# Hybrid decoder layer: the order of the norms at the seam between the first projections and the pairs, and of the first loads

## The chip, the cores and the metric

The kernel runs on one core of a Trainium2 chip. The metric is the device time of one execution in microseconds; a profiled execution shows where it goes. TensorE (PE in the profile) multiplies, VectorE (DVE) and ScalarE (ACT) prepare its operands and empty its banks, GpSimd (POOL) does side work and issues some transfers, and SyncE (SP) issues most transfers.

## The reference

One decoder layer on 512 tokens with 2048 features, in float32. What matters here is its front end:

```python
xn = rms_norm(x, attn_norm_g)          # per token, over 2048 features
proj = xn @ w_in                       # gq gk gv gg ga fq fk fv fg ff mq mg
...                                    # eight GLA heads, four FoX heads
mn = rms_norm(mem, mem_norm_g)         # 256 memory tokens
mk, mv = split(mn @ w_mem_kv)
...                                    # four heads of cross-attention over mem
h = x + (headnorm(o) * gate) @ w_out
y = h + relu(rms_norm(h) @ w_up) ** 2 @ w_down
```

The two norms that the change touches are those of x (one factor for each of 512 tokens) and of mem (one for each of 256). A norm's factor is a scale of a row, so the kernel multiplies with x and mem as they come and applies the factor when a result leaves its bank.

## The kernel before

Every product is made of three matmuls of 128 by 128 by 512 in a rounded format (`mm3`, L174 to L178): each operand is split into a high part (a copy on ScalarE) and a low part (the rest, a subtraction on VectorE).

The kernel is one sequence of stages on TensorE. The first projects two groups of columns, gk and gq (`project`, L232): eight rounds, in each of them two weight tiles and two tiles of x. The last of the sums of squares of x (xacc, L208) is ready long before its end. Then come four *pairs* (L513 to L515): `in_pair(n, c)` makes one half of the contraction (c) of two groups of 512 columns (n = 0: the GLA values, n = 1: the FoX queries and keys), in the order n, c = (0,0), (1,0), (0,1), (1,1). The text calls them first to fourth pair. A pair is a two-by-two block product in seven products instead of eight (Strassen with Winograd's sums): products p in the order 1, 5, 6, 3, 7, 2, 4 (L256), and each p is two steps q of 12 matmuls, so a pair has 14 steps or 168 matmuls. A weight block of a step is loaded (L311), perhaps combined with another block (`minus`, L472), and split into `hl` on ScalarE and VectorE (L367). There are four `hl` buffers, taken in turn: the split for a step starts when TensorE has left the step four before it. Names such as `hl_hl_in_51` say p = 5, q = 1.

After the last step of a product `evict` (L484) takes its two banks to the output o, with the factor of x's norm, r_x: on ScalarE (L492) the first time a place is written in the first two pairs, and on VectorE (L490) otherwise. Products 1, 6, 7 and 4 go on adding in the same two banks, so product 6 may start only when the eviction after product 1 is done; products 5 and 3 share another two.

Sums of blocks of x are an operand of products 5, 6, 3 and 7. For the first half of the contraction (c = 0) they are made during `project` and lie in sh (high) and sl (low). For c = 1 they are made by `x_sums(1)` (L427) in tiles xs (loads) and st (results) and parked in device memory by GpSimd (x_op, L442). During the second pair `next_sums` (L448) loads them back into sl, each when its product of the second pair is done, and splits them at once: the load, a copy on ScalarE, a subtraction on VectorE.

Beside that run the sums of squares of mem: 16 loads memT (L509), 16 squares on ScalarE (L219), 15 additions on VectorE (L220). `token_rstd` (L222) then multiplies with a column of ones (ss_x for x, ss_mem for mem; four and two small matmuls, L226), and `rsqrt` (L116) makes the factor in five small VectorE and two ScalarE operations. The program has, in this order: ss_x and r_x; x_sums(0); the squares of mem, then x_sums(1); ss_mem and its factor; the four pairs. The factor of mem is first used when mem's projections leave their banks, long after the pairs.

Two pools of buffers are shared: three `ta` tiles serve xraw, xs and memT in turn, four `tb` tiles serve the squares and st. Small banks of TensorE come from the pool of four `a` banks, in turn: gq has all four, then ss_x, ss_mem, product 5 of the first pair.

Where an instruction stands in its engine's queue is not the order of the text alone. A scheduler orders the program by priorities: `tc.high_priority(offset)` moves what it holds ahead, `urgent()` (L280) by twice the usual offset. Each engine then takes its queue strictly in order, SP's queue of transfers included: a transfer that waits for a buffer holds up all behind it.

Of the kernel before, what the change touches and what calls it, by code (L numbers as in the profile page):

```python
# [9 lines left out]
F32 = mybir.dt.float32  # L10
# [8 lines left out]
NT = S // 128  # L19
NK = D // 128  # L20
M = 256
MT = M // 128
# [16 lines left out]
AHEAD = 3000  # L39
# [8 lines left out]
def hybrid_layer(  # L48
# [17 lines left out]
    nc = tc.nc  # L66
    V, A, G, T = nc.vector, nc.scalar, nc.gpsimd, nc.tensor
# [26 lines left out]

    colt = const.tile([128, 68], F32, name="colt")
    with tc.high_priority(offset=AHEAD):
        nc.sync.dma_start(colt, cols)
    g_attn, g_mem, g_out, g_mlp = (colt[:, 16 * i : 16 * i + 16] for i in range(4))
    g_fq, g_fk, g_mq, g_mk = (colt[:, 64 + i : 65 + i] for i in range(4))

# [30 lines left out]
    def empty(evict, p, acc):  # L131
        traced = nc.cur_bb.bb.instructions
        last = traced[-1]
        with tc.high_priority(offset=2 * AHEAD):
            evict(p, acc)
        start = next(i for i in reversed(range(len(traced))) if traced[i] is last) + 1
        for engine in (V.engine, A.engine):
            emptied.extend([(turns["step"], i) for i in traced[start:] if i.engine == engine][-1:])
# [19 lines left out]
    def wtile(src, name, n=1024, parts=1):  # L158

        with tc.high_priority(offset=AHEAD):  # L160
            raw = wraw(turns["raw"] % 3, f"raw_{name}")
            turns["raw"] += 1
            both = hl_in(name, n_hl)
            hi, lo = both[:, :n], both[:, 1024 : 1024 + n]
            for i in range(parts):
                cs = slice(i * n // parts, (i + 1) * n // parts)
                nc.sync.dma_start(raw[:, cs], src[:, cs])
                A.copy(hi[:, cs], raw[:, cs])
                V.tensor_sub(lo[:, cs], raw[:, cs], hi[:, cs].bitcast(F32))
        return hi, lo  # L170
# [23 lines left out]
    def tmp(name, tag, n=512, dt=F32):  # L194
        return tp.tile([128, n], dt, tag=tag, name=name, bufs=TAGS[tag])
# [26 lines left out]
    def token_rstd(acc, n, name):  # L222

        ss = abank(f"ss_{name}")
        for t in range(n):
            T.matmul(ss[:, t : t + 1], lhsT=acc[:, t * 128 : t * 128 + 128], rhs=one_c, start=True, stop=True)  # L226
        r = const.tile([128, n], F32, name=f"r_{name}")
        rsqrt(r, ss[:, :n], n, 1.0 / D, name)
        return r


    def project(*groups):  # L232

        banks = [[(abank if i else gbank)(f"{g}_{t}") for t in range(NT)] for i, g in enumerate(groups)]
        for kp in range(NK // 2):
            for ps, group in zip(banks, groups):
                wh, wl = wtile(w_in[GROUPS.index(group), kp], f"{group}{kp}", parts=1 if kp else 2)
                for kk in range(2):
                    k = 2 * kp + kk
                    ah, al = x_tile(k)  # L240
                    for t in range(NT):
                        cs = slice(kk * 512 + t * 128, kk * 512 + t * 128 + 128)
                        mm3(ps[t], wh[:, cs], wl[:, cs], ah, al, k == 0, k == NK - 1)
        return [p for ps in banks for p in ps]
# [35 lines left out]
    def urgent():  # L280
        return tc.high_priority(offset=2 * AHEAD)
# [122 lines left out]


    kq = project("gk", "gq")
    xrstd = token_rstd(xacc, NT, "x")
    kTs = bigt(0, [128, NT, 512], "kTs")
    qTs = bigt(1, [128, NT, 512], "qTs")
    with urgent():  # L410
# [36 lines left out]

    def next_sums(n):  # L448
        hi, lo = sh[:, n, :, :], sl[n // 2][:, n % 2, :, :]
        nc.sync.dma_start(lo.bitcast(F32), x_op[n])  # L450
        A.copy(hi, lo.bitcast(F32))
        V.tensor_sub(lo, lo.bitcast(F32), hi.bitcast(F32))


    places = [[(1, 1), (1, 2)], [(0, 0), (0, 1)], [(0, 2), (1, 0)]]
# [1 line left out]
    class Pair(Weights):  # L457
# [16 lines left out]
        def left(self, p, j, u):  # L474
# [5 lines left out]
            at = u * 128 + (256 if p == 4 else 0)  # L480
            return xh[k][:, at : at + 128], xl[k][:, at : at + 128]

    def in_pair(n, c):
        def evict(p, acc):  # L484
            r, col = WHERE[p]
            for u in range(2):
                t = 2 * r + u
                dst = o[:, t, n * 1024 + col * 512 : n * 1024 + col * 512 + 512]
                if c or p in (3, 7, 2):
                    V.scalar_tensor_tensor(dst, acc[u], rs_x(t), dst, op0=ALU.mult, op1=ALU.add)  # L490
                else:
                    A.activation(dst, acc[u], AF.Copy, scale=rs_x(t))  # L492

        def after(p, acc):
            empty(evict, p, acc)
            if (c, n) == (0, 1) and p in SUMS:
                with tc.high_priority(offset=AHEAD):
                    next_sums(SUMS[p])

        multiply(Pair(n, c), after)  # L500

# [2 lines left out]

    macc = spare[:, 3072 : 3072 + M]
    with tc.issue_after(turned_kq[0].ins), tc.issue_after(turned_kq[1].ins):
        for k in range(NK):
            mt = tmp(f"memT_{k}", "ta", M)
            nc.sync.dma_start(mt, memT[k])  # L509
            add_squares(macc, mt, k == 0, f"mem{k}")  # L510
        x_sums(1)
    mrstd = token_rstd(macc, MT, "mem")
    for c in range(2):  # L513
        for n in range(2):
            in_pair(n, c)  # L515
    blocks.close()
    n_hl = 2
    turns["raw"] = 0
# [1059 lines left out]
```

## Time and profile before

| | us |
|---|---|
| median of 3 runs | 2128.58 |
| their range | 2126.21 to 2132.4 |
| the profiled execution | 2126.06 |
| its span, first to last instruction | 2124.0 |
| first matmul | 5.97 |
| first pair starts | 97.21 |
| fourth pair ends | 263.5 |

The profiled execution lies 0.15 below the lowest of the three runs. A row of the timeline gives the start, the time, engine, line, operation, output and inputs, the form, and in brackets the idle time before it and what ended that. A row of the chain gives start, length, engine and output. A row of a wait gives who waited for whom, the total, how often, and the longest. The windows give the busy time of each engine in a stretch.

### The profile page before, as it was taken

The page shows a single profiled execution, that of the slowest core. Times are in us where ns is not written, and L with a number is a line of the kernel's source. Part 1 is how long each engine was busy: PE and PEld are TensorE (multiplying, and loading weights), DVE is VectorE, ACT ScalarE, POOL GpSimd, SP SyncE. Part 2 cuts the span into 40 slices and gives each one's busy share as a digit, 9 for nine tenths or more (in the row PEclk, how much of TensorE's full clock was granted, in tenths as well). Part 3 has the DMA queues.
Part 4 walks back from the last instruction along what each step waited for, and adds up shares of the span by engine and source line. Part 5 has one row for each costly group of instructions (what it writes and reads, how often), then busy time and mean ns, then how long its engine had stood idle before and what let it go on. Part 6 is the DMA issues. An engine that isn't in the chain of part 4 may idle for free.

```text
span 2124.0 us, 25538 instructions
## 1 busy us (share of the span) xinstructions
PE 2100.5 (99%) x9746; PEld 1733.4 (82%) x9746; DVE 1615.4 (76%) x1747; ACT 1133.3 (53%) x1607; POOL 152.1 (7%) x220
## 2 busy tenths in 40 slices
PE   8999999999999999999999999999999999999999
PEld 7777878887788788888888888888888888888887
DVE  6579888764664899977777777778968868777875
ACT  6454364434563565755555555556646546556543
POOL 0012000000000022100000000000100000000000
PEclk9999999999999999999999999999999999999999
DMA  7355342121224666353353353355677668668653
GB/s 264 97 164 168 118 139 93 60 70 60 85 91 143 237 256 216 112 208 120 131 206 119 130 207 119 129 208 199 207 208 236 176 196 254 168 187 268 182 174 129
DMA packets 78755, 347.09 MB, mean 163 GB/s; under 512 B 9305, under 2 KB 13401, under 8 KB 57130
## 3 DMA queue, kind: packets, MB, share of 16 engines
q1 hardware_dynamic: 58778, 274.95, 37.1%
q0 software_dynamic: 19856, 70.53, 12.5%
q8 instruction: 76, 1.25, 0.2%
q14 instruction: 45, 0.37, 0.1%
HBM read 271.52 MB, written 73.92 MB: 163 GB/s over the span
## 4 chain that ended last, share of the span: by engine, by line
PE 95%; DVE 2%; DMA 1%; ACT 1%; issue 1%; SPq 0%; DVEq 0%; ACTq 0%
PE acc_up L177 9%; PE acc_up L178 9%; PE acc_up L176 9%; PE acc_dn L178 9%; PE acc_dn L177 9%; PE acc_dn L176 9%; PE acc_in L177 2%; PE acc_in L176 2%; PE acc_in L178 2%; PE acc_out L177 2%; PE acc_out L178 2%; PE acc_out L176 2%; PE gg L176 1%; PE gg L178 1%; PE gg L177 1%; PE ut L1394 1%
## 5 line engine op out<-in xcount | busy, mean ns | idle before, releaser
L367 DVE TENSOR_TENSOR hl_up<-raw_up,hl_up 128x1024 fp32r<-128x1024 f32 x224 | 273.0, 1223 | 141.0 <-ACT hl_up L367 139.6
L367 DVE TENSOR_TENSOR hl_dn<-raw_dn,hl_dn 128x1024 fp32r<-128x1024 f32 x224 | 272.8, 1222 | 125.0 <-ACT hl_dn L367 124.7
L367 ACT CAST hl_up<-raw_up 128x1024 fp32r<-128x1024 f32 x224 | 235.0, 1050 | 204.4 <-PE acc_up L178 136.0
L367 ACT CAST hl_dn<-raw_dn 128x1024 fp32r<-128x1024 f32 x224 | 234.7, 1053 | 195.5 <-PE acc_dn L178 146.5
L315 DVE TENSOR_TENSOR raw_dn<-raw_dn,raw_dn 128x2048 f32<-128x2048 f32 x64 | 146.3, 2286 | 0.4
L315 DVE TENSOR_TENSOR raw_up<-raw_up,raw_up 128x2048 f32<-128x2048 f32 (+1 forms) x62 | 140.6, 2267 | 0.0
L367 ACT CAST hl_out<-raw_out 128x1024 fp32r<-128x1024 f32 x56 | 58.0, 1050 | 48.8 <-PE acc_out L178 21.4
L1492 ACT COPY m<-acc_dn 128x512 f32<-128x512 f32 x96 | 55.7, 587 | 43.0 <-PE acc_dn L178 42.9
L1493 POOL DMA_DIRECT2D hd<-m x48 | 41.5, 865 | 515.5 <-ACT m L1492 515.5
L367 DVE TENSOR_TENSOR hl_out<-raw_out,hl_out 128x1024 fp32r<-128x1024 f32 x56 | 72.5, 1306 | 6.6 <-ACT hl_out L367 6.2
L367 ACT CAST hl_hl_in<-spare 128x1024 fp32r<-128x1024 f32 x31 | 32.3, 1050 | 51.3 <-DVE spare L472 30.0
L1386 POOL DMA_DIRECT2D op<-u x32 | 17.1, 535 | 559.5 <-ACT u L1395 554.6
L1409 ACT ACTIVATE z<-z,rstd 128x512 f32<-128x512 f32 x48 | 32.2, 716 | 44.9 <-DVE z L1458 44.9
L176 PE MATMUL acc_in<-hl_hl_in,sh 128*128 128x512 f32 x128 | 50.9, 400 | 2.8 <-ACT o L492 2.8
L176 PE MATMUL gg<-ahi_x,hl_gg 128*128 128x512 f32 x128 | 53.5, 418 | 0.0
L177 PE MATMUL acc_in<-hl_hl_in,sh 128*128 128x512 f32 x128 | 51.1, 399 | 0.0
L178 PE MATMUL acc_in<-hl_hl_in,sl 128*128 128x512 f32 x128 | 50.8, 397 | 0.0
L176 PE MATMUL acc_up<-hl_up,left0h 128*128 128x512 f32 x128 | 50.5, 394 | 0.0
L176 PE MATMUL acc_up<-hl_up,left5h 128*128 128x512 f32 x128 | 50.5, 394 | 0.0
L176 PE MATMUL acc_up<-hl_up,left1h 128*128 128x512 f32 x128 | 50.5, 394 | 0.0
L176 PE MATMUL acc_up<-hl_up,left2h 128*128 128x512 f32 x128 | 50.5, 394 | 0.0
L177 PE MATMUL acc_dn<-hl_dn,left 128*128 128x512 f32 x128 | 50.0, 391 | 0.4 <-DVE hl_dn L367 0.3
(542 smaller groups left out, 6245.2 us busy)
## 6 DMA issues: line engine op xcount, KB each, us to landing
raw_up<-in_w_up_dram SPq DMA_DIRECT2D x64, 1024.0 KB, 6.2
raw_dn<-in_w_down_dram SPq DMA_DIRECT2D x64, 1024.0 KB, 6.9
hd<-m POOLq DMA_DIRECT2D x48, 512.0 KB, 6.5
raw_out<-in_w_out_dram SPq DMA_DIRECT2D x16, 1024.0 KB, 5.8
op<-u POOLq DMA_DIRECT2D x32, 512.0 KB, 4.2
op<-s POOLq DMA_DIRECT2D x24, 512.0 KB, 3.1
spare<-in_w_pair_dram SPq DMA_DIRECT2D x16, 512.0 KB, 4.7
raw_in<-in_w_pair_dram SPq DMA_DIRECT2D x16, 512.0 KB, 4.1
```

The source lines that it names most:

```text
L176: T.matmul(ps, lhsT=ah, rhs=bh, start=start, stop=False, skip_group_check=on)
L177: T.matmul(ps, lhsT=ah, rhs=bl, start=False, stop=False, skip_group_check=on)
L178: T.matmul(ps, lhsT=al, rhs=bh, start=False, stop=stop, skip_group_check=on)
L315: V.tensor_sub(dst, a, b)
L367: turns["made"] = made = A.copy(hi, part), V.tensor_sub(lo, part, hi.bitcast(F32))
L1386: nc.gpsimd.dma_start(down_op[c][i][:, half * 1024 : half * 1024 + 1024], tile)
L1394: T.transpose(tps[:, m * 128 : m * 128 + 128], z[:, t * 512 + m * 128 : t * 512 + m * 128 + 128], ident)
L1409: A.activation(dst, src, AF.Relu, scale=rstd[:, 2 * row + t : 2 * row + t + 1])
L1492: A.copy(st[:, t * 512 : t * 512 + 512], acc[t])
L1493: nc.gpsimd.dma_start(dst, st.rearrange("p (t n) -> p t n", t=2), accum_op=ALU.add)
```

## The change

Five edits. The gains `colt` go out on GpSimd's queue instead of SP's. `project` asks for the first tile of x of a round ahead of that round's weights. The norm of x is put under `urgent`. The loads, squares and additions of mem stand behind the first pair in the program, and ss_mem with its factor behind all four. `next_sums` issues its load when its product is done, as before, but copy and subtraction are held back until the next product is done.

```diff
-        nc.sync.dma_start(colt, cols)
+        nc.gpsimd.dma_start(colt, cols)
...
         for kp in range(NK // 2):
             for ps, group in zip(banks, groups):
+                x_tile(2 * kp)
                 wh, wl = wtile(w_in[GROUPS.index(group), kp], f"{group}{kp}", parts=1 if kp else 2)
...
     kq = project("gk", "gq")
-    xrstd = token_rstd(xacc, NT, "x")
+    with urgent():
+        xrstd = token_rstd(xacc, NT, "x")
...
     def next_sums(n):
         hi, lo = sh[:, n, :, :], sl[n // 2][:, n % 2, :, :]
-        nc.sync.dma_start(lo.bitcast(F32), x_op[n])
-        A.copy(hi, lo.bitcast(F32))
-        V.tensor_sub(lo, lo.bitcast(F32), hi.bitcast(F32))
+        with tc.high_priority(offset=AHEAD):
+            nc.sync.dma_start(lo.bitcast(F32), x_op[n])
+
+        def landed():
+            A.copy(hi, lo.bitcast(F32))
+            V.tensor_sub(lo, lo.bitcast(F32), hi.bitcast(F32))
+
+        return landed
...
+    waiting_sums = []
...
         def after(p, acc):
             empty(evict, p, acc)
+            if waiting_sums:
+                waiting_sums.pop()()
             if (c, n) == (0, 1) and p in SUMS:
-                with tc.high_priority(offset=AHEAD):
-                    next_sums(SUMS[p])
+                waiting_sums.append(next_sums(SUMS[p]))
...
     with tc.issue_after(turned_kq[0].ins), tc.issue_after(turned_kq[1].ins):
-        for k in range(NK):
-            mt = tmp(f"memT_{k}", "ta", M)
-            nc.sync.dma_start(mt, memT[k])
-            add_squares(macc, mt, k == 0, f"mem{k}")
         x_sums(1)
-    mrstd = token_rstd(macc, MT, "mem")
     for c in range(2):
         for n in range(2):
             in_pair(n, c)
+            if not c and not n:
+                for k in range(NK):
+                    mt = tmp(f"memT_{k}", "ta", M)
+                    nc.sync.dma_start(mt, memT[k])
+                    add_squares(macc, mt, k == 0, f"mem{k}")
+    mrstd = token_rstd(macc, MT, "mem")
```

Since the scheduler decides the places, here is what stands in the queues at three of them. The first is TensorE's queue in the first pair; acc_in_1 are the banks of products 1 and 6, acc_in_5 those of product 5. Before:

```order
L177 MATMUL acc_in_1_1_983<-hl_hl_in_61_1078,sh 128x512
L178 MATMUL acc_in_1_1_983<-hl_hl_in_61_1078,sl_756 128x512
L226 MATMUL ss_mem<-wide,spare 128x1 [waits DVE_49,PE_49]
L226 MATMUL ss_mem<-wide,spare 128x1
L176 MATMUL acc_in_5_0_1018<-hl_hl_in_50_1025,sh 128x512 [waits PE_49]
L177 MATMUL acc_in_5_0_1018<-hl_hl_in_50_1025,sh 128x512
```

In the change, behind the last matmuls of product 1:

```order
L177 MATMUL acc_in_1_1_891<-hl_hl_in_11_909,ahi_x_223 128x512
L178 MATMUL acc_in_1_1_891<-hl_hl_in_11_909,alo_x_224 128x512
L176 MATMUL acc_in_5_0_926<-hl_hl_in_50_933,sh 128x512 [waits Activation_49]
L177 MATMUL acc_in_5_0_926<-hl_hl_in_50_933,sh 128x512 [waits DVE_49]
L178 MATMUL acc_in_5_0_926<-hl_hl_in_50_933,sl_756 128x512
```

Before, product 6 directly followed product 1, then ss_mem, then product 5. Now product 5 follows product 1, product 6 comes after it, and ss_mem stands behind the last matmul of the fourth pair.

The second place is VectorE's queue at the same time, from the first operation on ss_x to the factor r_x; z_x are steps on the way. Before:

```order
L119 TENSOR_SCALAR s_x<-ss_x 128x4
L367 TENSOR_TENSOR hl_hl_in_51_1041<-spare,hl_hl_in_51_1041 128x1024
L472 TENSOR_TENSOR raw_in_010_1020<-raw_in_110_1058,raw_in_010_1020 128x1024
L122 TENSOR_TENSOR z_x<-y_x 128x4
L367 TENSOR_TENSOR hl_hl_in_60_1062<-spare,hl_hl_in_60_1062 128x1024
L472 TENSOR_TENSOR spare<-spare 128x1024
L123 TENSOR_TENSOR z_x<-z_x,s_x 128x4
L220 TENSOR_TENSOR spare<-spare,sq_mem_831 128x256
L124 TENSOR_SCALAR z_x<-z_x 128x4
L220 TENSOR_TENSOR spare<-spare,sq_mem_836 128x256
L125 TENSOR_TENSOR r_x<-y_x,z_x 128x4
```

In the change:

```order
L122 TENSOR_TENSOR z_x<-y_x 128x4
L123 TENSOR_TENSOR z_x<-z_x,s_x 128x4
L124 TENSOR_SCALAR z_x<-z_x 128x4
L125 TENSOR_TENSOR r_x<-y_x,z_x 128x4
L368 TENSOR_TENSOR hl_hl_in_51_949<-spare,hl_hl_in_51_949 128x1024
```

Six other operations stood between the steps of r_x; now none does, and s_x directly precedes these rows. On TensorE the four matmuls of ss_x, which followed the last of gq, now stand five matmuls before it.

The third place is ScalarE's queue at the end of the first pair; sq_mem are squares of mem, xs a tile for x_sums(1), hl_40 and hl_41 the last two operands of the first pair, hl_10 the first of the second. In the change:

```order
L435 ACTIVATE xs_1_875<-xs_1_875,colt 128x512 [waits DMAHW3_49,DVE_49,Activation_49]
L368 CAST hl_hl_in_21_1089<-spare 128x1024 [waits DMAHW2_49,PE_49,Activation_49]
L216 ACTIVATE spare<-memT_1140 128x256 [waits DMAHW5_49]
L368 CAST hl_hl_in_40_1107<-spare 128x1024 [waits DVE_49,PE_49,Activation_49]
L219 ACTIVATE sq_mem_1145<-memT_1143 128x256 [waits DMAHW7_49,DMASW3_49,DMASW1_49]
L219 ACTIVATE sq_mem_1150<-memT_1148 128x256 [waits DMAHW0_49,DMASW4_49,DMASW2_49]
L219 ACTIVATE sq_mem_1155<-memT_1153 128x256 [waits DMASW7_49,DMASW6_49,DMAHW1_49,DMASW5_49,DVE_49]
L219 ACTIVATE sq_mem_1160<-memT_1158 128x256 [waits DMAHW2_49,DMASW7_49,DMASW0_49]
L368 CAST hl_hl_in_41_1123<-spare 128x1024 [waits DVE_49,PE_49,Activation_49]
L368 CAST hl_hl_in_10_1224<-raw_in_000_1220 128x1024 [waits PE_49,Activation_49]
```

Before, the squares of mem stood at the first pair's start:

```order
L219 ACTIVATE sq_mem_836<-memT_834 128x256 [waits DMAHW1_49]
L367 CAST hl_hl_in_60_1062<-spare 128x1024 [waits PE_49]
L219 ACTIVATE sq_mem_841<-memT_839 128x256 [waits DMAHW5_49]
L219 ACTIVATE sq_mem_846<-memT_844 128x256 [waits DMAHW6_49]
L219 ACTIVATE sq_mem_851<-memT_849 128x256 [waits DMAHW7_49,DVE_49,Activation_49]
L219 ACTIVATE sq_mem_856<-memT_854 128x256 [waits DMAHW0_49,DVE_49,Activation_49]
L492 ACTIVATE o<-acc_in_1_0_982,r_x 128x512 [waits DVE_49,PE_49]
```

The squares now begin between the last splits of the first pair and run through the middle of the second. Four of them wait for transfers of GpSimd's queue (DMASW), the writes of x_op that empty the shared `tb` tiles. In SP's queue the 16 loads of mem now stand among the weight loads of the second pair, the last eight in a row ahead of its last two weight tiles. Behind the pairs, from some 30 us after their end to the end of the kernel, the queues are the same as before.

## Prediction

> **What bounds the kernel now.** I read the page first.
>
> ```profile
> span 2124.0 us, 25538 instructions
> PE 2100.5 (99%) x9746; PEld 1733.4 (82%) x9746; DVE 1615.4 (76%) x1747; ACT 1133.3 (53%) x1607; POOL 152.1 (7%) x220
> ```
>
> TensorE is busy for 99% of the span, so only time in which it stands still, or runs at half its clock, can be won. The change reorders work up to about 290 us, so next I read TensorE's own waits from 0 to 330 us. These are all of them above 0.9 us:
>
> ```profile
> PE gk L176 <- ACT ahi_x L186: 6.0, 1, 6.0
> PE ss_mem L226 <- DVE spare L220: 3.4, 1, 3.4
> PE acc_in L177 <- DVE hl_hl_in L367: 2.8, 2, 1.8
> PE acc_in L176 <- ACT o L492: 2.8, 1, 2.8
> ```
>
> One is the start, the others lie in the first two pairs. The timeline of TensorE shows what they cost:
>
> ```profile
> 102.56 0.39 PE L178 MATMUL acc_in<-hl_hl_in,alo_x 128*128 128x512 f32 x1
> 105.70 0.50 PE L176 MATMUL acc_in<-hl_hl_in,sh 128*128 128x512 f32 x1 [2.76 <-ACT o L492]
> 111.05 0.39 PE L178 MATMUL acc_in<-hl_hl_in,sl 128*128 128x512 f32 x1
> 114.82 0.90 PE L226 MATMUL ss_mem<-wide,spare 128*128 128x1 f32 x4 [3.38 <-DVE spare L220]
> 115.59 0.77 PE L176 MATMUL acc_in<-hl_hl_in,sh 128*128 128x512 f32 x1
> 121.71 0.41 PE L178 MATMUL acc_in<-hl_hl_in,sl 128*128 128x512 f32 x1
> 121.96 0.40 PE L176 MATMUL acc_in<-hl_hl_in,sh 128*128 128x512 f32 x1
> 178.52 0.39 PE L176 MATMUL acc_in<-hl_hl_in,ahi_x 128*128 128x512 f32 x1
> 179.92 0.50 PE L177 MATMUL acc_in<-hl_hl_in,ahi_x 128*128 128x512 f32 x1 [1.01 <-DVE hl_hl_in L367]
> 182.54 0.39 PE L176 MATMUL acc_in<-hl_hl_in,ahi_x 128*128 128x512 f32 x1
> 184.68 0.50 PE L177 MATMUL acc_in<-hl_hl_in,ahi_x 128*128 128x512 f32 x1 [1.75 <-DVE hl_hl_in L367]
> ```
>
> The pitch without a wait comes from the windows by pair (stretch, length; then busy time of PE, PEld, DVE, ACT and POOL with their instructions; granted clock, DMA share, GB/s):
>
> ```profile
> 97.20:145.40 48.20, 42.06 (x172) 33.87 (x172) 35.14 (x56) 26.56 (x45) 3.43 (x6) 0.93 0.53 164
> 145.40:186.30 40.90, 38.14 (x167) 30.94 (x166) 36.63 (x42) 24.59 (x31) 18.67 (x35) 1.00 0.60 199
> 186.30:224.50 38.20, 38.20 (x170) 31.60 (x169) 35.04 (x39) 15.61 (x17) 0.00 (x0) 1.00 0.39 122
> ```
>
> The third pair takes 38.20 us without a gap: over 168 matmuls 0.227 each, over 14 steps 2.73. The first took 48.2 (granted clock 0.93, the others 1.00), the second 40.9.
>
> **The stalls, one by one.** Their chain, from the rows of the chain of waits:
>
> ```profile
> 104.57 0.08 DVE r_x L125
> 104.98 1.25 ACT o L492 x2
> 108.40 2.06 DMA memT<-in_memT_dram
> 114.25 0.43 DVE spare L220
> ```
>
> *A, 102.8 to 105.7.* Product 6 waits for the eviction after product 1, and that for r_x, whose last step ended only at 104.65 though ss_x was multiplied here:
>
> ```profile
> 96.40 0.95 PE L226 MATMUL ss_x<-wide,xacc 128*128 128x1 f32 x8
> ```
>
> The next matmul was due at 102.56 + 0.23 = 102.79; lost 2.91, and 0.11 in a longer first matmul (0.34 to the next): 3.0.
>
> *B, 111.3 to 114.8.* ss_mem waits for the additions of mem, and these for memT's loads. Due at 111.28: lost 3.5 (ss_mem's own 0.8 is not won, it moves behind the pairs).
>
> *C, 115.6 to 122.* After B the matmuls come 0.43 apart. From 115.59 to 121.96 there are 15: 6.37 us against 15 x 0.227 = 3.40, lost 3.0. Gap A, 2.9 long, left the clock as it was; gap B, 3.5 long, halved it. The Trainium skill ("TensorE: Matmul & The Clock Gate", Part 1) says the same of the threshold, about 3.4 us of idling, but gives about 3.4 us for the way back, where the rows show over 6; by its figure C would cost 1.7 and the sum below be 1.3 smaller.
>
> *D, at 178.75 and 182.77.* Two late splits: 179.92 - 178.75 = 1.17 and 184.68 - 182.77 = 1.91, with two longer first matmuls (0.1 each) 3.3. They come from the sums for c = 1:
>
> ```profile
> 170.91 0.63 ACT L541 ACTIVATE rows_r<-wide 36x512 fp32r<-36x512 f32 x1 [4.53 <-DMA x_op<-st]
> 172.51 1.23 DVE L452 TENSOR_TENSOR sl<-sl,sh 128x1024 fp32r<-128x1024 f32 x1 [2.23 <-ACT sh L451]
> 179.98 1.05 ACT L451 CAST sh<-sl 128x1024 fp32r<-128x1024 f32 x1 [3.10 <-DMA sl<-x_op]
> ```
>
> ScalarE waited 4.53 for the last writes of x_op and later 3.10 for a reload, with the splits of the pair queued behind on ScalarE, and behind its copies on VectorE.
>
> A + B + C + D = 3.0 + 3.5 + 3.0 + 3.3 = **12.8**.
>
> **What each edit does to them.** *The norm of x ahead.* In the queues of the change r_x follows s_x with nothing between, and ss_x starts five matmuls earlier, near 95.3. Its bank must first be emptied of gq's first result; the bound is 0 to 0.2 on TensorE and I take 0.1, nothing in the sum. r_x is then ready near 98.5, where the first eviction is due at 102.8. And product 5 now stands between products 1 and 6: two steps, 5.4 us, cover that eviction (1.25 in the row above). A goes; what is late next is the split of product 5's second operand, which ScalarE starts some 1.2 later than before (its y_x steps come first), near 98.3; split by about 100.5, used at 97.2 + 3 x 2.73 = 105.4. Covered.
>
> *Squares of mem behind the first pair, ss_mem behind all.* B goes and C with it. The work itself moves: 16 squares, 15 additions, 16 loads. From VectorE's groups in the first pair, where all 15 lay:
>
> ```profile
> L220 DVE TENSOR_TENSOR spare<-spare,sq_mem 128x256 f32<-128x256 f32 x15 | 6.4, 425 | 2.9 <-ACT sq_mem L219 2.0
> L263 DVE TENSOR_TENSOR st<-xs,xs 128x256 f32<-128x256 f32 x2 | 0.8, 422 | 0.5 <-ACT xs L433 0.5
> ```
>
> In the change three additions stay in the first pair and twelve (5.1) go to the second; x_sums(1) comes forward, ten of its sixteen additions (4.2) from the second pair to the first. VectorE then has 35.1 - 5.1 + 4.2 = 34.2 in the first pair and 36.6 + 5.1 - 4.2 = 37.5 in the second, each of 38.2. The third pair has 35.0 and TensorE never waits. So the first pair is covered, and the second is full to 98%: a stall there is bounded by 0 (the four hl buffers let a split be three steps, 8.2, early, of which cast and subtraction take some 2.3) and by 37.5 + the 4.3 that VectorE idled in the second pair before - 38.2 = 3.6. ss_mem's two matmuls (0.8) and its short chain move to about 263, 30 us and more ahead of their first use; covered.
>
> *The reload's split held back by a product.* The load has two steps, 5.4, to land instead of none; its wait on ScalarE (3.10) goes, and x_op is written earlier, so the 4.53 goes too. D goes.
>
> *New waits.* On ScalarE four squares of mem wait for the last writes of x_op, with hl_41 of the first pair and hl_10 of the second queued behind. GpSimd's writes of x_op take (the second row is the landing of all transfers of x_op, the reloads among them):
>
> ```profile
> L442 POOL DMA_DIRECT2D x_op<-st x16: 542/542/721, 118.4 to 165.5; - x16
> DMA to landing us min/median/max: 2.0/3.8/6.6
> ```
>
> The last st tiles are due near 123 to 124.5 in the new order; four issues of 0.54 and 3.8 of landing put those squares near 129 to 130, hl_41 is split by about 132.4, and TensorE wants it at 97.2 + 13 x 2.73 = 132.7. That is just enough; with 6.6 it would be 2.5 late. In SP's queue loads of mem wait for squares with weights behind them; their weights are wanted 4 us and more after they land. I take 1.3 for all new stalls of the pairs, near the lower bound, since the third pair's row (35.0 of 38.2, no stall) is the nearest.
>
> *The start.* The chain and the timeline, then the landings of colt and of xraw's transfers up to 30 us:
>
> ```profile
> 0.81 0.39 SPq L97 DMA_DIRECT2D colt<-in_cols_dram  x1
> 1.72 3.39 DMA xraw<-in_xT_dram
> 5.19 0.73 ACT ahi_x L186
> 5.82 0.61 ACT L216 ACTIVATE xacc<-xraw 128x512 f32<-128x512 f32 x1
> 6.34 0.60 ACT L168 CAST hl_gk<-raw_gk 128x512 fp32r<-128x512 f32 x1
> ...
> DMA to landing us min/median/max: 1.8/1.8/1.8
> ...
> DMA to landing us min/median/max: 2.6/3.6/5.8
> ```
>
> x is issued at 0.81 instead of 1.72 and with the same 3.39 lands at 4.2. But ScalarE's queue now is ahi_x, xacc, hl_gk; before, hl_gk came first, while x was still under way. From the start of ahi_x to a split hl_gk are 0.63 + 0.52 + 0.60, so the first matmul starts at 4.3 + 1.75 + 0.06 = 6.1 instead of 5.97; if x lands after 2.6, the shortest of its transfers, at 5.3. I take 5.8, **0.2** won. That needs colt by 4.2. On SP it took 1.8; on GpSimd's queue, issued near 0.8 for 0.72, with 2.0 to 6.6 of landing it is there between 3.5 and 8.1. The small read is nearest to the lower end. The Trainium skill speaks against this edit ("DMA: Bandwidth & Descriptors", Specifications): GpSimd's path brings its first byte after about 1 us, SP's after 0.6; by that colt comes 0.4 later than on SP, still ahead of x, and the sum stays.
>
> **Sum:** 12.8 + 0.2 - 1.3 = 11.7, so the profiled execution would take 2126.06 - 11.7 = 2114.4. The median of the three runs lies 2.5 above it: 2128.58 - 11.7 = 2116.9. I forecast the median, 2117.
>
> **Rivals.** *1, the second pair fills up:* VectorE at 98% and the squares on ScalarE give a new stall of 3.6, just long enough to halve the clock once more (3.0, as C). Won: 12.8 + 0.2 - 6.6 = 6.4, median 2122. For it: the 98%; against: the lead of hl_50 and later ones is two steps. *2, colt is late:* at 8.1 the first matmul starts 3.9 later, at 10.0 instead of 6.1. Won: 12.8 - 1.3 - 4.0 = 7.5, median 2121. For it: the 6.6 landing; against: those were writes to device memory beside other traffic. *3, slower:* in the second pair loads and squares of mem run in rounds of three `ta` tiles. A round costs a landing, 2.06, plus issue and three squares, about 3.6 together, in which ScalarE's queue holds the splits. It decides from where the splits' lead is used up; if then three rounds each show as a gap that halves the clock, three times 3.6 + 3.0 = 19.8 against 13.0 won: 6.8 slower, median 2135. For it: before, 13 loads took from 98.6 to 113.7 in just this way; against: TensorE ran through most of that. *4, the seam only moves:* the norm's chain still ends late and most of A and B reappears elsewhere; won under 6, median 2124. The queues speak against it.
>
> **Chances.** Forecast 0.67, rival 1 0.14, rival 2 0.09, rival 3 0.04, rival 4 0.06. The forecast's own range is 0 to 3.6 of new stalls and 0.5 either way at the start, with the runs' spread of about 2 below and 4 above: 2113 to 2120. To leave out no more than 2 in 10 the range takes in rivals 1 and 2: **2113 to 2123**. A measurement of this kernel can tell about 0.3%, 6.4 us, from no change. Faster by more: the forecast, rival 2 (0.09) and half of rival 1, 0.83; within it: half of rival 1 and rival 4, 0.13; slower: 0.04.
>
> **What would show it.** Right: no gap above 1 us between 97 and 190, granted clock 1.00 in the first pair, product 5 behind product 1, each of the first two pairs near 38.2 to 39.5 us, first matmul near 5.8. Wrong: a wait of TensorE on hl_41 or hl_10 near 132 with ScalarE waiting for x_op; colt as the releaser of ahi_x; matmuls 0.43 apart after 13 us; waits for hl in the third pair, which would say that the second's debt is only passed on.

## The result, and the profile after

The changed kernel takes 2118.13 us, the median of 4 runs (2116.60 to 2119.36), beside 2129.55 for the kernel before (4 runs, 2126.21 to 2132.40): a ratio of 0.9947, interval 0.9929 to 0.9964. The medians differ by 11.4; the forecast was 11.7 and 2117. In the later batches of runs the kernel before had medians of 2127.10, 2127.63 and 2127.49 (9 to 15 runs), and the changed kernel, run again, 2117.23: there the difference is 10.3. The two profiled executions differ by less, 2126.06 - 2119.36 = 6.7: the profiled run of before was its fastest, that of after its slowest.

The page of the changed kernel, its first lines:

```profile
span 2117.6 us, 25529 instructions
PE 2098.0 (99%) x9746; PEld 1730.3 (82%) x9746; DVE 1614.6 (76%) x1747; ACT 1132.0 (53%) x1607; POOL 151.7 (7%) x221
```

TensorE's own waits in the changed kernel, up to the end of the pairs:

```profile
PE gk L176 <- ACT hl_gk L168: 7.2, 1, 7.2
PE acc_in L177 <- DVE hl_hl_in L368: 1.8, 4, 0.6
```

The waits for ss_mem and for o are gone, and the two late splits of 1.0 and 1.8 are four of at most 0.6. One row became worse: the first matmul starts at 7.20, not at 5.97. The rows of the start (GpSimd's issue of colt, ScalarE, the first matmul, and the first that is again 0.23 from the next):

```profile
1.36 0.69 POOL L97 DMA_DIRECT2D colt<-in_cols_dram  x1 [0.85 <-POOLq L1579]
5.40 0.72 ACT L186 ACTIVATE ahi_x<-xraw,colt 128x512 fp32r<-128x512 f32 x1 [3.31 <-DMA colt<-in_cols_dram]
7.20 0.79 PE L176 MATMUL gk<-ahi_x,hl_gk 128*128 128x512 f32 x1 [7.20 <-ACT hl_gk L168]
11.18 0.39 PE L176 MATMUL gk<-ahi_x,hl_gk 128*128 128x512 f32 x1
```

x landed 2.7 after its issue at 0.81; the gains were issued at 1.36 and took 4.0, and ScalarE waited for them. But the half clock ended at 11.18 here and at 12.47 before, so the first pair still starts at 97.23 (97.21 before).

At the seam the last step of r_x starts at 98.06, 6.4 earlier than before (104.49 in this view); product 1 is evicted at once, and TensorE goes on with product 5:

```profile
98.06 0.16 DVE L125 TENSOR_TENSOR r_x<-y_x,z_x 128x4 f32<-128x4 f32 x1
101.65 0.69 ACT L501 ACTIVATE o<-acc_in,r_x 128x512 f32<-128x512 f32 x1
102.68 0.39 PE L176 MATMUL acc_in<-hl_hl_in,sh 128*128 128x512 f32 x1
```

The windows by pair, columns as before, each from a pair's first matmul to the next pair's. The granted clock is 1.00 throughout. A pair without a wait takes 38.08 (in e7 below all four do), so the four lose 0.8, 1.5, 0.4 and 0.8:

```profile
97.23:136.11 38.88, 38.42 (x169) 31.47 (x168) 31.82 (x47) 25.29 (x38) 8.60 (x16) 1.00 0.68 219
136.11:175.69 39.58, 38.73 (x169) 31.40 (x168) 37.80 (x47) 26.41 (x37) 12.54 (x25) 1.00 0.56 190
175.69:214.14 38.45, 38.37 (x169) 31.47 (x168) 35.36 (x36) 15.28 (x16) 0.00 (x0) 1.00 0.31 110
214.14:252.97 38.83, 38.38 (x169) 31.47 (x168) 35.15 (x38) 14.12 (x14) 0.96 (x1) 1.00 0.29 98
```

By stages, before to after: start to first pair 0.0; the four pairs 166.3 to 156.1 (up to the next stage's first matmul, with ss_mem's 0.4 now behind them), 10.2 won; from there to the first matmul of the last large stage ("down", acc_dn) 1245.0 to 1245.1; from that to the end of the span 615.5 to 619.2, 3.7 lost. 10.2 - 3.7 = 6.5 is the difference of the spans, 2124.0 - 2117.6 = 6.4, within 0.1. The queues of the down stage are the same in both kernels; the last run below asks whether that loss is the change's.

### The profile page after: what moved, and what is told of

The parts are those of the page before. It is cut to its first block, busy times and chain, and to the rows that moved or that the text cites. A ratio compares the mean times of both kernels' runs of the same rounds, so it can differ in the third digit from the quotient of the medians.

```text
span 2117.6 us, 25529 instructions
## 1 busy us (share of the span) xinstructions
PE 2098.0 (99%) x9746; PEld 1730.3 (82%) x9746; DVE 1614.6 (76%) x1747; ACT 1132.0 (53%) x1607; POOL 151.7 (7%) x221
## 3 DMA queue, kind: packets, MB, share of 16 engines
q0 software_dynamic: 19888, 70.56, 12.4%
## 4 chain that ended last, share of the span: by engine, by line
PE 91%; DVE 5%; DMA 2%; ACT 1%; issue 1%; ACTq 0%; SPq 0%; DVEq 0%; POOLq 0%
PE acc_up L177 10%; PE acc_up L178 10%; PE acc_up L176 9%; PE acc_dn L177 9%; PE acc_dn L178 9%; PE acc_dn L176 9%; PE acc_out L177 2%; PE acc_out L178 2%; PE acc_out L176 2%; PE gg L176 1%; PE gg L178 1%; PE gg L177 1%; DVE hl_hl_in L368 1%; PE ut L1405 1%; PE lp L820 1%
## 5 line engine op out<-in xcount | busy, mean ns | idle before, releaser
L1504 POOL DMA_DIRECT2D hd<-m x48 | 41.4, 863 | 519.3 <-ACT m L1503 519.3
L177 PE MATMUL acc_in<-hl_hl_in,sh 128*128 128x512 f32 x128 | 50.1, 391 | 0.5 <-DVE hl_hl_in L368 0.4
L177 PE MATMUL acc_dn<-hl_dn,left3h 128*128 128x512 f32 x128 | 50.1, 392 | 0.4 <-DVE hl_dn L368 0.4
L177 PE MATMUL acc_up<-hl_up,left 128*128 128x512 f32 x128 | 50.1, 391 | 0.2 <-DVE hl_up L368 0.2
```

What stands on the lines that cost most here:

```text
L177: T.matmul(ps, lhsT=ah, rhs=bl, start=False, stop=False, skip_group_check=on)
L1504: nc.gpsimd.dma_start(dst, st.rearrange("p (t n) -> p t n", t=2), accum_op=ALU.add)
```

## The experiments

The theory: the gain is made in the four pairs alone, and mostly by the memory's move. The rivals are the prediction's own reading, in which each edit takes its stall away, and its first rival, a VectorE too full in the second pair. All marks below are read from the timelines. The half clock is the time from the first matmul to the first that is again about 0.23 from the next; the four pairs run from their first matmul to the first of the next stage. A ratio compares a kernel with the runs of before in its own batch, whose medians were 2127.10 (e1 to e4), 2127.63 (e5 to e8) and 2127.49 (e9 to e12).

| kernel | first matmul | half clock | four pairs | down stage | median | ratio to before, interval |
|---|---|---|---|---|---|---|
| before | 5.97 | 6.50 | 166.3 | 615.5 | 2129.55 | |
| after | 7.20 | 3.98 | 156.1 | 619.2 | 2118.13 | 0.9947 (0.9929-0.9964) |
| e1 norm back | 6.30 | 3.15 | 154.7 | 618.9 | 2117.25 | 0.9949 (0.9934-0.9964) |
| e2 memory back | 6.93 | 3.58 | 164.4 | 617.8 | 2126.33 | 0.9994 (0.9984-1.0003) |
| e3 sums back | 6.98 | 5.71 | 156.6 | 619.2 | 2119.53 | 0.9960 (0.9946-0.9974) |
| e4 memory only | 5.91 | 3.94 | 156.4 | 616.1 | 2117.41 | 0.9949 (0.9934-0.9964) |
| e5 start back | 5.76 | 5.22 | 154.8 | 618.6 | 2116.77 | 0.9947 (0.9935-0.9960) |
| e6 gains on ScalarE | 5.62 | 5.22 | 155.1 | 618.0 | 2115.70 | 0.9943 (0.9930-0.9957) |
| e7 memory in third | 6.98 | 3.57 | 152.7 | 616.2 | 2114.04 | 0.9934 (0.9920-0.9947) |
| e8 spread + e6 | 5.70 | 3.94 | 154.1 | 615.7 | 2113.76 | 0.9932 (0.9920-0.9945) |
| e9 e7 + e6 | 5.60 | 4.83 | 153.2 | 618.1 | 2114.36 | 0.9934 (0.9922-0.9946) |
| e10 e9, two edits less | 5.73 | 5.71 | 155.1 | 617.4 | 2114.97 | 0.9940 (0.9926-0.9953) |
| e11 sums only | 5.80 | 3.94 | 164.4 | 618.8 | 2125.42 | 0.9993 (0.9984-1.0002) |
| e12 change again | 6.98 | 4.43 | 153.9 | 619.0 | 2117.23 | 0.9955 (0.9943-0.9968) |

672 matmuls at 38.08 for 168 are 152.3, and ss_mem behind them 0.4, so a pair column of 152.7 has no stall in it.

**Which edit takes A, B and C away: e1, e2 and e4.** e1 undoes the norm's place in the changed kernel:

```diff
-    with urgent():
-        xrstd = token_rstd(xacc, NT, "x")
+    xrstd = token_rstd(xacc, NT, "x")
```

> The changed kernel with the norm of x no longer put ahead; all else as changed. Theory 1: what took stall A away is the place of product 5 between products 1 and 6, and that comes from the memory's sum leaving the queue, not from the norm's early factor. r_x is then late again, near 104.7, and its eviction is done by about 107.4, but product 6 is wanted only at 97.2 + 4 x 2.73 = 108.1: no gap at 102.8, the pairs end within 0.5 us of the change's 253.3, the time is the same (within 1 us of 2118). Theory 2, the prediction's: the early factor carries A; the pairs end 3 us later, near 256.3, with a wait of TensorE on o.

The rows of e1: r_x is late again and the eviction waits 2.75 for it, but that delays no matmul, since product 5 covers it. These two rows are the eviction and all that TensorE waited for in the pairs:

```profile
103.31 1.27 ACT L500 ACTIVATE o<-acc_in,r_x 128x512 f32<-128x512 f32 x2 [2.75 <-DVE r_x L125]
PE acc_in L177 <- DVE hl_hl_in L368: 1.2, 2, 0.7
```

The pairs end at 250.6, earlier than either theory gave: they start 1.4 before the change's and lose 1.4 less. But no matmul waits for o: that is the mechanism of theory 1, and the early factor is worth nothing here. e2 puts the memory back in its old place, with all other edits kept:

```diff
     with tc.issue_after(turned_kq[0].ins), tc.issue_after(turned_kq[1].ins):
+        for k in range(NK):
+            mt = tmp(f"memT_{k}", "ta", M)
+            nc.sync.dma_start(mt, memT[k])
+            add_squares(macc, mt, k == 0, f"mem{k}")
         x_sums(1)
+    mrstd = token_rstd(macc, MT, "mem")
...
-            if not c and not n:
...
-    mrstd = token_rstd(macc, MT, "mem")
```

> The changed kernel with the memory's loads, squares and sum back in their old place; all else as changed. Theory 1: stalls A and B of before were in series, and the memory's loads end near 114 whatever TensorE does, so with r_x early there is no gap at 102.8, but the wait for the memory's sum starts near 108.3 and is about 6 us long (3.5 + 2.9), the clock halves behind it (3.0), and the small stalls at 133, 167 and 173 (1.8 in all) go: the pairs end 7 to 9 us later than 253.3, at 260.5 to 262.5. Theory 2: the stalls are independent; the gap is 3.5, with 3.0 at half clock: 4.5 to 6.5 later, at 258 to 260.

TensorE in e2, the last matmul before the wait, ss_mem, and the first matmul that is again 0.23 from the next; then the last additions of mem on VectorE:

```profile
107.89 0.39 PE L178 MATMUL acc_in<-hl_hl_in,sl 128*128 128x512 f32 x1
114.52 0.98 PE L226 MATMUL ss_mem<-wide,spare 128*128 128x1 f32 x4 [6.25 <-DVE spare L220]
119.77 0.40 PE L177 MATMUL acc_in<-hl_hl_in,sh 128*128 128x512 f32 x1
113.42 0.95 DVE L220 TENSOR_TENSOR spare<-spare,sq_mem 128x256 f32<-128x256 f32 x2 [0.73 <-ACT sq_mem L219]
```

A is gone and its 2.9 us are found again in B: ss_mem starts at 114.52 (114.82 before), whatever TensorE did in between, because the memory's loads, and with them its additions, end then. The stalls were in series on two independent chains; the shorter one alone was worth nothing. The pairs end 7.9 later than in the change, as theory 1 has it, and of 166.3 only 1.9 are won. The first pair took even 50.2 (48.7 before), with four short waits besides the long one, 2.6 in all. The second ran without a wait in 38.1, so D's 3.4 are won in full, though the memory is in its old place. e4 is the opposite, the kernel before with the memory's move alone:

```diff
-        for k in range(NK):
...
         x_sums(1)
-    mrstd = token_rstd(macc, MT, "mem")
     for c in range(2):
         for n in range(2):
             in_pair(n, c)
+            if not c and not n:
+                for k in range(NK):
...
+    mrstd = token_rstd(macc, MT, "mem")
```

> The kernel before with nothing but the memory's move. Theory 1: this alone brings product 5 between 1 and 6 and takes A, B and C away: 9.5 less the new stalls of 1.3 to 2.6; D stays (3.3) or half of it. The pairs end at 263.5 - 9.5 + 2 = 256, between 254.5 and 257.5; first matmul at 5.97 as before. Theory 2: without the early factor A stays: the pairs end 3 us later than that, near 259.

156.4 us of pairs (they end at 252.4, even before the expected 254.5, since they start at 96.0) and a median 10 below before: the gain within the spread, with r_x at 103.2. Nothing else of the change is needed for A, B and C.

**The reloaded sums: e3 and e11.** e3 splits them at once in the changed kernel; e11 is the kernel before with nothing but the held-back split, the same lines the other way round.

```diff
...
             empty(evict, p, acc)
-            if waiting_sums:
-                waiting_sums.pop()()
             if (c, n) == (0, 1) and p in SUMS:
-                waiting_sums.append(next_sums(SUMS[p]))
+                with tc.high_priority(offset=AHEAD):
+                    next_sums(SUMS[p])
```

> The changed kernel with the reloaded sums split at once again; all else as changed. Theory 1, the prediction's D: each of the four reloads takes 4 to 7 us, and copy and subtraction in the queues ahead of the pair's splits hold these up; 3.3 us or more come back in the second pair (more, if the memory's squares in the same pair take away the lead that splits had): pairs end at 256.5 to 258. Theory 2: D came only from the late writes of x_op (the wait of 4.53), which the change issues earlier by moving the memory; then 1 us or less comes back, 254.3 at most.

> The kernel before with nothing but the held-back split of the reloaded sums. Theory 1: D comes from the late writes of x_op, the memory's squares in the first pair push them there, and a split held for one product of 5.4 us covers only part: of the two stalls at 178.75 and 182.77 (1.17 and 1.91) at least one stays or moves, 0 to 2 us are won of 3.3. Theory 2, the prediction's: holding back alone takes D away, the pairs take 163.0 instead of 166.3.

e3's pairs take 156.6; the five kernels with the change's memory place and held splits (after, e1, e5, e6, e12) take 153.9 to 156.1, mean 154.9. So the held split is worth about 1.6 there, less than theory 1 asked and more than theory 2; from one profile of e3, and with 2.2 between the five, that is a rough figure. In e11 one of the two stalls of D stays, the other goes (166.3 to 164.4): theory 1. The rows of e11, ScalarE and TensorE:

```profile
169.49 0.63 ACT L549 ACTIVATE rows_r<-wide 36x512 fp32r<-36x512 f32 x1 [4.54 <-DMA x_op<-st]
181.37 0.50 PE L177 MATMUL acc_in<-hl_hl_in,ahi_x 128*128 128x512 f32 x1 [1.01 <-DVE hl_hl_in L367]
```

The wait of 4.54 for x_op's writes is untouched by holding back. D had two causes: the split at once, 1.6 to 1.9 of its 3.3, and the late writes, the rest. These go with the memory's move, but not with it alone: in e2, with the memory in its old place, the last write of x_op was issued at 159.2 (164.0 in e11, 165.5 before), no wait for it is left, and D is gone. e2 differs from e11 by the norm's place and the start; which of them brings the writes forward was not separated.

**The start: e5 and e6.** e5 undoes both edits of the start (first piece), e6 moves only the gains, to ScalarE's queue (second piece):

```diff
-        nc.gpsimd.dma_start(colt, cols)
+        nc.sync.dma_start(colt, cols)
...
-                x_tile(2 * kp)
```

```diff
-        nc.gpsimd.dma_start(colt, cols)
+        nc.scalar.dma_start(colt, cols)
```

> The changed kernel with both edits of the start undone (the gains on SyncE's queue, the weights ahead of x). Theory 1: GpSimd's queue issues the gains at 1.36 and they land 3.1 to 4.0 later, so the changed start is the worse one; undone, the first matmul is at 5.9 to 6.0 instead of 6.3 to 7.2. The half clock then lasts 3.4 to 6.5 from there, as in the other profiles, so the first pair starts between 95.5 and 97.5 and the time cannot tell the two (within 2 us of 2118). The down stage (from its first matmul to the end of the span: 619.2, 618.9, 617.8 and 619.1 in the four profiles with the changed start, 615.5 and 616.1 in the two without) stays between 617 and 620, if it is chance. Theory 2: the changed start also moves all later transfers by one place among the queues, and that costs 3 us in the down stage; undone, the stage takes 616 and the time falls by 3.

> The changed kernel with the gains issued by ScalarE's queue instead of GpSimd's; x stays ahead of the weights. Theory 1: x lands at 3.4 to 3.5 in the changed kernel and only the gains are late, so with the gains there by 3.4 the first scaled tile starts near 3.5 and the first matmul is at 5.3 (the lower end that the prediction gave), 1 to 1.9 earlier than in the four profiles of the changed start; in the time the chance of the half clock's end hides it. Theory 2: ScalarE's queue first loads its tables (0.80 to 2.08 in the changed kernel) or issues late, the gains come near 4.2 or later, and the first matmul is at 6.0 or later.

The first scaled tile in e5, and the gains' issue, the first scaled tile and the first matmul in e6:

```profile
4.99 0.72 ACT L186 ACTIVATE ahi_x<-xraw,colt 128x512 fp32r<-128x512 f32 x1 [0.34 <-DMA xraw<-in_xT_dram]
```

```profile
0.81 0.41 ACTq L97 DMA_DIRECT2D colt<-in_cols_dram  x1
3.82 0.72 ACT L186 ACTIVATE ahi_x<-xraw,colt 128x512 fp32r<-128x512 f32 x1 [1.30 <-DMA colt<-in_cols_dram]
5.62 0.80 PE L176 MATMUL gk<-ahi_x,hl_gk 128*128 128x512 f32 x1 [5.62 <-ACT hl_gk L168]
```

In e5 the tile waits for x, in e6 for the gains still. First matmul: 5.76 to 5.97 with the old start (4 profiles), 6.30 to 7.20 with the gains on GpSimd (6), 5.60 to 5.73 with them on ScalarE (4). So the changed start is about 1.0 later than the old one. e6 came between its two theories: 5.62, not 5.3, since the gains issued beside x took 3.0 on this queue too, against 1.7 to 1.9 as the first transfer of SP's queue. So GpSimd's queue accounts for only part of the delay: it issues 0.55 later and takes 0.1 to 1.0 longer than ScalarE's. In all 14 profiles the first pair starts at 87.9 to 88.2 plus the first matmul's time plus half of the half clock, so that 1.0 would be lost one for one. No median tells these differences: the half clock's 3.15 to 6.50 moves the first pair by half of the difference, up to 1.7, from one execution to the next. The down stage of e5 is as long as in the change, so theory 1 holds there.

**Is a full VectorE the limit: e7 and e8.** e7 queues the memory's work one pair later, behind the last split made (first piece; `turns["made"]` holds its two operations); e8 gives it out one square to each product (second piece), and has the gains on ScalarE's queue as in e6:

```diff
-            if not c and not n:
+            if not c and n:
+                last = turns["made"]
+                with tc.issue_after(last[0].ins), tc.issue_after(last[1].ins):
...
```

```diff
...
             if waiting_sums:
                 waiting_sums.pop()()
+            if waiting_mem and (c or n):
+                k = waiting_mem.pop(0)
+                mt = tmp(f"memT_{k}", "ta", M)
+                nc.sync.dma_start(mt, memT[k])
+                last = turns["made"]
+                with tc.issue_after(last[0].ins), tc.issue_after(last[1].ins):
+                    add_squares(macc, mt, k == 0, f"mem{k}")
...
```

> The changed kernel with the memory's loads, squares and additions one pair later: queued behind the last split of the second pair, so that 12 of the 15 additions fall into the third. It tests the prediction's rival of a full VectorE. By the busy times the third pair would have 34.9 + 5.1 = 40.0 us of VectorE work in 38.2: if VectorE's sum sets the pair, TensorE loses at least 1.8 us there and the waits are on VectorE's splits. The second pair then has 32 us, and the waits at 133.4 (for memT on ScalarE) and 173 go. Rival: the waits of after were of queue places, not of the sum (the second pair ran with 37.2 of 39): the third pair passes some of its work on to the fourth and loses under 1 us; the pairs end within 1 us of 253.3 less the difference at the start.

> The changed kernel with two edits: the gains on ScalarE's queue as in the run before, and the memory's 16 squares given out one behind each product from the second pair on, each queued behind that product's splits, instead of all in a row. Theory 1: the four small waits of the pairs (1.8, with their longer first matmuls 2.3) come from the row of squares and the loads behind it; spread, at most 1 is left (the one at 167, for a reload of the sums), and the four pairs take 154.5 to 155 instead of 156.1: 1 to 1.5 us won, with the earlier start 2 to 3 (2115 to 2117). Rival: the waits move with the squares, since each still stands in ScalarE's queue among the splits: 156 as in the change.

The second and third pair of e7, then the second of e12, which is the changed kernel once more (last run below):

```profile
134.90:172.98 38.08, 38.08 (x169) 31.53 (x168) 34.69 (x35) 26.10 (x33) 0.00 (x0) 1.00 0.53 180
172.98:211.06 38.08, 38.08 (x169) 31.53 (x168) 37.62 (x47) 18.42 (x27) 0.00 (x0) 1.00 0.45 141
```

```profile
135.38:173.59 38.21, 38.21 (x169) 31.43 (x168) 37.74 (x47) 26.44 (x37) 14.75 (x25) 1.00 0.56 196
```

VectorE is busy for 37.62 of 38.08 in the third pair of e7, and TensorE waits nowhere in the four. In e12 it is busy for 37.74 of 38.21 in the second, and that pair loses 0.1. So the sum of VectorE's work was not what made the second pair of the changed kernel 39.58 long, with 37.80 of it. What did stands in its ScalarE queue: there a copy of a reloaded sum waits for its load, with splits behind it, and TensorE waits for a split soon after. The first pair has the same with squares that wait for memT. The rows of the second pair, then of the first:

```profile
163.32 1.05 ACT L456 CAST sh<-sl 128x1024 fp32r<-128x1024 f32 x1 [3.79 <-DMA sl<-x_op]
167.01 0.51 PE L177 MATMUL acc_in<-hl_hl_in,ahi_x 128*128 128x512 f32 x1 [0.58 <-DVE hl_hl_in L368]
```

```profile
128.20 0.42 ACT L219 ACTIVATE sq_mem<-memT 128x256 f32<-128x256 f32 x1 [2.92 <-DMA memT<-in_memT_dram]
130.77 0.42 ACT L219 ACTIVATE sq_mem<-memT 128x256 f32<-128x256 f32 x1 [1.19 <-DMA memT<-in_memT_dram]
133.44 0.50 PE L177 MATMUL acc_in<-hl_hl_in,ahi_x 128*128 128x512 f32 x1 [0.46 <-DVE hl_hl_in L368]
```

In e12 the same copy starts at 161.07 and the same last square at 130.08, and neither wait of TensorE is there: whether the loads land in time differs from one execution to the next. In e7 the squares stand behind the splits, and no wait is left: theory 1 of e7 falls, and its rival does even better than expected. e8's pairs, 154.1, keep two waits of 0.47 and 0.33, where 1 was allowed; spreading is no better than the right place.

**The best found: e9 and e10.** e9 is e7 with e6's edit; e10 has the same two on the kernel before, with x ahead of the weights, but without the norm ahead and with the sums split at once, each by its diff above.

> The changed kernel with the memory's squares queued behind the last split of the second pair (as in e7) and the gains on ScalarE's queue (as in e6): the best of what the runs so far point to. Theory: the two add up. First matmul 5.6 (7.0 in e7), the four pairs 152.7 as in e7 with no wait above 0.3, so 1.0 to 1.4 less than e7's 2114.0: a median of 2112.5 to 2113.5, and 4 to 6 less than the changed kernel run beside it. Rival: the half clock at the start ends when it will (3.15 to 6.5 after the first matmul), so the earlier start buys nothing that shows: 2114, as e7.

> The kernel before with three edits only: the memory's squares queued behind the last split of the second pair, its sum behind all pairs, and the first x ahead with the gains on ScalarE's queue. The norm of x is not put ahead, and the reloaded sums are split at once. Theory 1: those two edits do nothing once the memory is out of the first pair; the pairs take 152.7 to 153.5 and the time is within 1 us of the run before this. Theory 2: the sums split at once meet the memory's squares at the start of the third pair, and the norm's steps stand among splits in the first: 1 to 3 us of new waits, pairs 154 to 156.

e9's pairs take 153.2 and its median of 2114.36 is no better than e7's 2114.04, so the start's 1.4 doesn't show: that is the rival's outcome, and the spread of the runs (2109.40 to 2116.29) can't exclude the other. All three of e7, e8 and e9 have lower ratios to before than the change (0.9932 to 0.9934, against 0.9947 and, in e12, 0.9955), though the intervals overlap. e9 ran beside e12, the change itself, and is 2.9 lower, with none of its runs above the lowest of e12's. e10 has one wait that e9 lacks, on VectorE's split at the start of the third pair:

```profile
PE acc_in L177 <- DVE hl_hl_in L368: 1.7, 1, 1.7
```

That is 1.9 us of pairs. Splitting at once is the likely cause, since e3 and e4, which do the same, each have a wait of 0.89 at that product too, and the kernels that hold back have none there; it was not separated from the norm's place.

**What repeats: e12.** The changed kernel, unaltered.

> The changed kernel once more, unaltered, beside the others. It measures what two profiles of one kernel differ by: the half clock at the start (4.0 long in the first profile), the four pairs (156.1 there; 154.8 and 155.1 in two kernels with the same pairs), the down stage (619.2 there; 615.5 to 619.1 in the nine others). Theory: all three are chance, so here the pairs take 154.5 to 156.5, the down stage lies anywhere between 615.5 and 619.2, and the median is 2117 to 2118.5. Rival: the 619.2 belongs to this kernel and comes again.

TensorE's waits in the pairs and in the down stage of e12, then the down stage of after and of e7:

```profile
PE acc_in L177 <- DVE hl_hl_in L368: 0.4, 1, 0.4
PE acc_dn L177 <- DVE hl_dn L368: 1.8, 6, 0.3
```

```profile
PE acc_dn L177 <- DVE hl_dn L368: 2.3, 7, 0.4
```

```profile
PE acc_dn L177 <- DVE hl_dn L368: 0.6, 2, 0.3
```

The pairs of one and the same kernel took 156.1 and then 153.9, and the median is within 1 us of the first: chance, as the theory says. The down stage is the rival's: 619.2 came again as 619.0. But the old start does not cure it (e5 618.6, e11 618.8), nor does the changed start always have it (e7 616.2). The change has seven waits of up to 0.4 on splits there, 2.3 in all, and the kernel before one of 0.3, so they are 2.0 of the 3.7. What decides how many there are stays open, and of the kernel before there is only one profile.

## Why the prediction was right, point by point

- **The sum over the pairs** was 12.8 - 1.3 = 11.5, so 154.8 for the four. Measured: 156.1 in the profile shown, 153.9 in the repeat, 154.9 in the mean of five. Right, but closer than its terms: without a stall the pairs take 152.7, so there were 13.6 to win and not 12.8, and the new stalls cost 2.2 in the mean and not 1.3. The two errors cancel. (The prediction's windows also cut the pairs early: these start at 97.21, 145.88 and 187.32, so the first two took 48.7 and 41.4.)
- **A.** "A goes" was right, and the place of product 5 was named; but the early factor was given a share in it. e1 shows that it has none, and e2 that A alone wins nothing while B stands: the two were in series, so their worth could only be added because both went.
- **B and C** went, as worked out. The reading behind C failed: "gap A, 2.9 long, left the clock as it was; gap B, 3.5 long, halved it" is no rule of lengths. In e11 a gap of 2.9 at the same place did halve the clock (last section).
- **D** was right in size. It was put to the reload's split with the earlier x_op beside it; e11 and e3 give the first 1.9 and 1.6, and the rest went where x_op was written earlier (e2, and with the memory's move).
- **New stalls**: 1.3 was taken. Against 152.7 without a stall the five kernels lose 1.2 to 3.4, 2.2 in the mean. hl_41 was late as feared, in the first profile, but by 0.46 and for memT's landing, not for the writes of x_op; in the repeat it was in time.
- **The start** is the term that was wrong: "0.2 won" with the first matmul at 5.8. It came at 7.20, and at 6.9 in the mean of six. The step that failed is "the small read is nearest to the lower end": on GpSimd's queue the gains were issued at 1.36, not 0.8, and took 3.1 to 4.0; beside x they took 3.0 on ScalarE's queue too. So rival 2 was real at a third of its price. In the two profiles the half clock gave it back by chance.
- **Rival 1** had its condition met in e12 and e7 (VectorE at 99% of a pair), and no stall followed.
- **Behind the pairs** the sum had no term, but the down stage was 3.7 longer in the profile shown and 3.5 in the repeat. Against the 10.2 to 12.4 won in the pairs the medians show 11.4 and 10.3 won, so that 11.4 came within 0.3 of the forecast is partly luck.

## What to carry to other kernels

Two waits of one engine on two independent chains are in series: price them together, and expect nothing from removing the earlier one while the later chain ends at its own time. Before giving an engine's fill as the limit, look at what stands ahead of the urgent work in its queue: an operation that waits for a load holds up more than the microseconds it is busy. And when a gain is a few microseconds, read it from a stage's length in several profiles; one profile of before and one of after differed here by nearly 4 us in a stage whose queues are the same in both.

## What the runs showed of the hardware

The half clock, in which matmuls come 0.43 apart instead of 0.23, begins and ends on a grid of time; the length of a gap alone does not decide it. In e11 the matmuls came 0.43 apart from the first one to 9.74, from 105.40 to 108.81, and again up to 119.10:

```profile
9.74 0.44 PE L178 MATMUL gk<-ahi_x,hl_gk 128*128 128x512 f32 x1
101.23 0.39 PE L178 MATMUL acc_in<-hl_hl_in,alo_x 128*128 128x512 f32 x1
104.37 0.50 PE L176 MATMUL acc_in<-hl_hl_in,sh 128*128 128x512 f32 x1 [2.75 <-ACT o L499]
105.40 0.62 PE L177 MATMUL acc_in<-hl_hl_in,sh 128*128 128x512 f32 x1
108.81 0.40 PE L176 MATMUL acc_in<-hl_hl_in,sh 128*128 128x512 f32 x1
119.10 0.39 PE L178 MATMUL acc_in<-hl_hl_in,sl 128*128 128x512 f32 x1
```

(105.40 - 9.74) / 28 = 3.416, (108.81 - 9.74) / 29 = 3.416, (119.10 - 9.74) / 32 = 3.418: all changes lie on one grid of 3.42 us. On it the gap from 101.46 to 104.37 takes 2.4 of one window (102.0 to 105.4), and the next window ran at half. In the kernel before the grid through 12.47 cuts a gap of the same length at 104.7 into 1.9 and 1.0, and the clock stayed; its C, 115.0 to 121.8 on that grid, was two windows: the 128x512 matmuls came back only at 115.59, 0.6 into the first. In e11 they came back at 115.60, just ahead of that grid's 115.7, and one window was enough. At the start the full clock comes with the end of the first window that the matmuls filled: in e1 0.27 was missing at its beginning and it counted, in the kernel before 0.33 was missing and one more went by (read to a matmul, some 0.2 to 0.4). So the half clock at the start lasts one to two windows, as the grid happens to lie: the 14 profiles lie between 3.15 and 6.50. The Trainium skill ("TensorE: Matmul & The Clock Gate", Part 1) describes a free-running window of 3.413 us, and the rows agree; the spread of half a microsecond either way that it gives for the turn is far below the one measured here.
